# Two sums over channels by a pair of fp32r products, and the layer norm's mean one unit later

## The chip, the cores and the metric

The kernel runs on one core of one Trainium2 chip. The metric is the time of one execution on the device, in microseconds (us). The engines are called as the profile calls them: PE is TensorE (matrix products), PEld its weight load, DVE is VectorE, ACT is ScalarE, POOL is GpSimd and SP is SyncE, which here issues most of the transfers. PSUM is the memory that TensorE accumulates into; it is handed out in banks of 128x512 fp32.

## The reference

One encoder layer over 512 positions of 2048 channels, in fp32. After an RMS norm one projection feeds two groups: a convolution module with a layer norm, and neighbourhood attention with 16 heads. Each group's output is divided by its root mean square, and both go through one output projection. A gated MLP follows.

```
h = u_val * sigmoid(u_gate)
h = depthwise_conv(h, dw_w, dw_b)                # width 31, 1024 channels
mu = mean(h); var = mean(square(h - mu))         # over channels
y_conv = silu((h - mu) * rsqrt(var + EPS) * ln_g + ln_b)

y_na = neighborhood_attention(q, k, v, rpb)      # 1024 channels
mixed = concat(rms_norm(y_conv, conv_out_g), rms_norm(y_na, na_out_g))
x = x + mixed @ w_out
x = x + (silu(gate) * val) @ w_down              # from x's norm, w_up and a width-3 convolution
return rms_norm(x, final_norm_g)
```

The change touches the mean of the layer norm, and the root mean square of the attention's output.

## The kernel before, in words

Activations stand with channels on the 128 partitions and the 512 positions along the free side, so 1024 channels are eight tiles of 128x512. A mean over channels is therefore a sum over tiles, done by VectorE, and then a sum over partitions, done by TensorE with a matrix of ones.

**Products.** Weights come as raw fp32 units of 128x1024. ScalarE makes a high part in the format fp32r (L130), VectorE the rest (L131). Activations are split in the same way. A unit of the projections is 24 products of 128x512: high by high and high by low for eight tiles, alternating (L147, L148), then low by high (L150). The first projection takes two such units for one block of 128 output columns, the output projection one (`out_half`, L602), first for the convolution's half and then for the attention's.

**Steps between units.** What lies between projections, such as attention, layer norm and roots, is written as coroutines. `tick` (L157) is called behind the last product of each unit; it runs the coroutine at the head of `steps` and the one at the head of `asteps` up to their next `yield`. So a `yield` moves what follows it one unit later. Attention of a head pair is such a coroutine in `steps`: scores, some units later the transposes of the softmax (L522), a unit later the products with the values (L538). `group_a`, in `asteps`, is the layer norm and what follows it: the sum of the eight convolution tiles (L426, L428), the mean (L431, L433), deviations and squares (L436, L437), the inverse root of the variance, normalising, swish and the split of the operands (L443 to L445), and five units later the group's own root (`ra`, L451). `norm_b` (L614) makes the attention group's root `rna` from `acc_na`, the sum of its squares.

**Order.** A planner puts the instructions of each engine in order when the program is built, by their places in the program (moved by `shifted`), by their dependences and by its own estimates of time; it also hands out the buffers. `issue_after` and `pin` bind the order in places. On the chip each engine then runs its list in that order.

**Roots.** `rsqrt_steps` (L254) sums over partitions with a narrow product for each block of 128 positions (L258), so that positions come to lie on partitions. `root_steps` makes the inverse root on tiles of 128x4 (L233 to L240), builds diagonal blocks (L245), and a unit later spreads them over all partitions with two products of ones (L249) and a copy (L251).

**Buffers.** `stat` (L222) takes PSUM for such sums from a tile of two banks with the tag `sc`, which is shared with attention's scores, transposes and value products; there is one of it. Projections rotate through three banks (`psm`). A unit of the output projection is read from its bank when `ra` is there (`read_a`, L617 to L623), in the second half with `rna` (L652). Small tiles of 128x512 come from a pool of 75. Weights are loaded into nine buffers, four of which hold the convolution's results until the layer norm has read them.

Of the kernel before, what the change touches and what calls it, by code (L numbers as in the profile page):

```python
# [10 lines left out]
F32 = mybir.dt.float32  # L11
F32R = mybir.dt.float32r
AF = mybir.ActivationFunctionType
ALU = mybir.AluOpType
AX = mybir.AxisListType

P = 128
D = 2048
S = 512
# [4 lines left out]
NA = 1024  # L24
# [4 lines left out]
EPS = 1e-6  # L29
# [49 lines left out]
def layer(ctx: ExitStack, tc: tile.TileContext, xT, xn, xw, w_0, w_in, w_out, w_up, w_down, par, tab, g3, out):  # L79
    nc = tc.nc  # L80
# [6 lines left out]
    psa = ctx.enter_context(tc.tile_pool(name="psa", bufs=1, space=bass.MemoryType.PSUM))  # L87
# [9 lines left out]
    def t2(name, dt=F32):  # L97
        return tp.tile([P, S], dt, tag="t2k", name=name)
# [8 lines left out]
    def pc(name, i):  # L107
        o = POFF[name] + i
        return prm[:, o:o + 1]

    ones_r = consts.tile([P, P], F32R, name="ones")
    ones = ones_r.bitcast(F32)
# [3 lines left out]
    ps = psm.tile([P, S], F32, tag="mm", name="warm")  # L116
# [5 lines left out]
    def raw_unit(src, n):  # L122
        raw = t4([P, U * P], "raw")
        return raw, nc.sync.dma_start(raw[:, :n], src)
# [82 lines left out]
    def split(src, g, name):  # L207

        h, l = t2(name + "h", F32R), t2(name + "l", F32R)
        nc.scalar.activation(h, src, AF.Copy, scale=g)  # L210
        nc.vector.scalar_tensor_tensor(l, src, g, h.bitcast(F32), op0=ALU.mult, op1=ALU.subtract)
        return h, l

    def sum_sq(acc, src, first, to=slice(0, S)):
        if first:
            nc.scalar.activation(acc, src, AF.Square)
        else:
            q = t2("sq")[:, to]
            nc.scalar.activation(q, src, AF.Square)
            nc.vector.tensor_add(acc, acc, q)  # L220

    def stat():  # L222
        if where:
            return psa.tile([P, S], F32, tag="tr", name="st", bufs=2)
        return psa.tile([P, 2, S], F32, tag="sc", name="st")[:, 0]
# [3 lines left out]
    def root_steps(sums, n, name, bank=None):  # L229

        v, r, y = (sm.tile([P, S // P], F32, tag="rs" + c, name="rs" + c) for c in "vry")
        h = sm.tile([P, S // P], F32R, tag="rsh", name="rsh")
        nc.vector.tensor_scalar(v, sums, 1.0 / n, EPS, op0=ALU.mult, op1=ALU.add)  # L233
        nc.scalar.activation(r, v, AF.Sqrt)
        nc.vector.tensor_mul(y, r, r)
        nc.vector.tensor_add(y, y, v)
        nc.vector.reciprocal(y, y)
        nc.vector.scalar_tensor_tensor(y, y, 2.0, r, op0=ALU.mult, op1=ALU.mult)
        nc.vector.tensor_copy(h, y)
        nc.vector.tensor_sub(v, y, h.bitcast(F32))  # L240

        dg = [t2("dg", F32R) for _ in range(2)]
        for d, x in zip(dg, (h.bitcast(F32), v)):
            for i in range(S // P):
                nc.vector.tensor_scalar(d[:, i * P:(i + 1) * P], ident, x[:, i:i + 1], None, op0=ALU.mult)  # L245
        yield
        ps = bank() if bank else stat()
        for i in range(2):
            nc.tensor.matmul(ps, ones_r, dg[i], start=i == 0, stop=i == 1)  # L249
        res = t2(name)  # L250
        nc.scalar.activation(res, ps, AF.Copy)  # L251
        return res

    def rsqrt_steps(acc, n, name, bank=None):  # L254

        ps = stat()
        for i in range(S // P):
            nc.tensor.matmul(ps[:, i:i + 1], acc[:, i * P:(i + 1) * P], ones[:, 0:1], start=True, stop=True)  # L258
        return (yield from root_steps(ps[:, :S // P], n, name, bank))


    xs, x1 = [], []
    pin = tc.keep_in_program_order

# [25 lines left out]
    for k in range(ROWS):  # L290
        n = 3 * P
# [8 lines left out]
        else:  # L300
            his = [t2("weh", F32R)[:, :P], t2("weh", F32R)[:, P:n]]
            h, l = t2("xh", F32R), t2("xl", F32R)
# [22 lines left out]
    for u in range(2):  # L325
        raw, i = raw_unit(w_in[1, :, u * U * P:(u + 1) * U * P], U * P)
# [8 lines left out]
    for step in ORDER:  # L335
        i = next(a_ if step == "a" else q_)
# [84 lines left out]
    def group_a():  # L421
        yield
        while taps:
            yield
        acc = t2("acc")
        nc.vector.tensor_add(acc, ys[0], ys[1])  # L426
        for i in range(2, NC_):
            nc.vector.tensor_add(acc, acc, ys[i])  # L428
        yield
        ps = psa.tile([P, 2, S], F32, tag="sc", name="st")[:, 0]  # L430
        nc.tensor.matmul(ps, ones, acc, start=True, stop=True)  # L431
        mu = t2("mu")
        nc.vector.tensor_scalar(mu, ps, 1.0 / CONV, None, op0=ALU.mult)  # L433
        acc = t2("acc")
        for i in range(NC_):
            nc.vector.tensor_sub(ys[i], ys[i], mu)  # L436
            sum_sq(acc, ys[i], i == 0)  # L437
        yield
        yield
        r = yield from rsqrt_steps(acc, CONV, "rln")  # L440
        acc = t2("acc")
        for i in range(NC_):
            nc.vector.tensor_mul(ys[i], ys[i], r)  # L443
            nc.scalar.activation(ys[i], ys[i], AF.Silu, scale=pc("lng", i), bias=pc("lnb", i))
            ma.append(split(ys[i], pc("cog", i), "ma"))  # L445
        for i in range(NC_):
            sum_sq(acc, ys[i], i == 0)
        for _ in range(RA_AFTER):
            yield

        ra.append((yield from rsqrt_steps(acc, CONV, "ra",  # L451
                                          lambda: psa.tile([P, S], F32, tag="po", name="st"))))


    mb, rb = [], []
    acc_na = t2("accna")
# [123 lines left out]
    p, n = -1, 0  # L580
    for step in ORDER:
        if step == "a":
            if n < 2:
                with tc.issue_after(last.ins):
                    glu(n) if n else first_glu()
            else:
                glu(n)
            n += 1
            continue
        p += 1  # L590
        steps.append(attend(p, *qkv(p)))
        if p == NORM_AT:
            asteps.append(group_a())
# [18 lines left out]
    wait = []  # L612

    def norm_b():  # L614
        rb.append((yield from rsqrt_steps(acc_na, NA, "rna")))

    def read_a(d, ps):  # L617
        wait.append((d, ps))
        while ra and wait:
# [3 lines left out]
            nc.vector.tensor_add(x2[d], x2[d], t)  # L623

    steps.append(norm_b())
    assert len(ma) == NC_
    out_half(ma, read_a)
# [465 lines left out]
```

## Time and profile before

| what | us |
|---|---|
| median of 3 runs | 1960.12 |
| lowest and highest | 1960.04 and 1960.94 |
| the profiled execution | 1960.14 |
| its span in the trace | 1958.4 |
| TensorE busy | 1948.2 (99%) |
| VectorE busy | 1605.9 (82%) |
| ScalarE busy | 1084.3 (55%) |

The span is the time between the first and the last recorded instruction; the execution's time has 1.74 us around it. A row of the chain gives a start, a length and the work; a row of a timeline adds the idle time of the engine ahead of it, with what ended that. A row of the windows gives a stretch, its length, and the busy times of TensorE, its weight load, VectorE, ScalarE and POOL, then the granted clock and the load of the transfers. A row of waits gives who waited for whom, the total, how often and the longest.

### The profile page before, as it was taken

The numbers are of one execution on the slowest core, as the hardware profiler recorded it, in microseconds if no ns is written. First come the engines' busy times: TensorE is split into PE (matmuls) and PEld (weight loads), VectorE is DVE, ScalarE is ACT, GpSimd is POOL, SyncE is SP. The second block draws the span as 40 slices with busy tenths as digits, with TensorE's granted clock in tenths as the row PEclk, the third lists the DMA queues.
The fourth block names the chain that finished last, engine by engine and source line by source line (L and its number), as shares of the span: only waits on it lengthen the run. The fifth ranks groups of instructions, "written<-read, shape, count | busy, mean of one in ns | idle before, by whom it ended". The sixth has DMA issues, their size and how long they took to land.

```text
span 1958.4 us, 28132 instructions
## 1 busy us (share of the span) xinstructions
PE 1948.2 (99%) x10391; PEld 1657.4 (85%) x10391; DVE 1605.9 (82%) x2348; ACT 1084.3 (55%) x1724; POOL 225.8 (12%) x310
## 2 busy tenths in 40 slices
PE   9999999999999999999999999999999999999998
PEld 8888888888888888888888888888888888888886
DVE  5988688887548888888888888898989898885764
ACT  6244423448426666666666666666666644554654
POOL 0111111110011111111111111111111300000000
PEclk9999999999999999999999999999999999999999
DMA  9677677677768899999999999999996967666663
GB/s 372 177 188 182 188 190 182 184 182 234 240 161 218 198 258 253 267 249 265 246 264 249 263 257 255 259 253 259 252 259 166 389 233 234 218 215 194 192 204 118
DMA packets 141531, 448.92 MB, mean 229 GB/s; under 512 B 14928, under 2 KB 27216, under 8 KB 139984
## 3 DMA queue, kind: packets, MB, share of 16 engines
q1 hardware_dynamic: 89168, 291.90, 44.0%
q0 software_dynamic: 42624, 148.92, 35.4%
q10 hardware_dynamic: 9600, 6.29, 1.1%
q8 instruction: 82, 1.34, 0.3%
q14 instruction: 57, 0.47, 0.1%
HBM read 428.17 MB, written 111.15 MB: 275 GB/s over the span
## 4 chain that ended last, share of the span: by engine, by line
PE 99%; DVE 1%; issue 0%; ACT 0%; DVEq 0%
PE pu L749 44%; PE pd L888 21%; PE pj L147 7%; PE pj L148 7%; PE pj L150 7%; PE po L147 3%; PE po L148 3%; PE po L150 3%; PE pj L386 1%; PE po L538 1%; PE pj L390 1%; PE sc L497 1%; PE trp L522 1%; PE trx L644 0%; DVE acc L428 0%
## 5 line engine op out<-in xcount | busy, mean ns | idle before, releaser
L130 ACT ACTIVATE whi<-raw 128x1024 fp32r<-128x1024 f32 (+1 forms) x574 | 604.3, 1054 | 535.8 <-PE pj L148 134.6
L131 DVE TENSOR_TENSOR wlo<-raw,whi 128x1024 fp32r<-128x1024 f32 (+1 forms) x574 | 698.9, 1218 | 221.4 <-ACT whi L130 194.1
L749 PE MATMUL pu<-xc,whi 128*128 128x512 f32 x2464 | 593.6, 391 | 0.0
L749 PEld LDWEIGHTS pu<-xc,whi 128*128 128x128 f32 x2464 | 451.3, 188 | 86.7 <-DVE xc L637 0.4
L749 PEld LDWEIGHTS pu<-xc,wlo 128*128 128x128 f32 x2464 | 319.2, 191 | 13.7
L749 PE MATMUL pu<-xc,wlo 128*128 128x256 f32 x2464 | 324.2, 283 | 0.0
L888 PE MATMUL pd<-whi,ho 128*128 128x512 f32 x1232 | 305.1, 389 | 0.0
L888 PEld LDWEIGHTS pd<-whi,ho 128*128 128x128 f32 x1232 | 231.1, 188 | 48.7 <-DVE vl L762 0.5
L147 PE MATMUL pj<-xh,whi 128*128 128x512 f32 x592 | 233.2, 394 | 0.0
L148 PE MATMUL pj<-xl,whi 128*128 128x512 f32 x592 | 230.8, 390 | 0.0
L413 DVE SCALAR_TENSOR_TENSOR y<-ch,prm,y 128x500 f32<-128x500 f32 (+14 forms) x240 | 177.1, 741 | 5.3
L888 PE MATMUL pd<-wlo,ho 128*128 128x512 f32 x616 | 165.1, 389 | 0.0
L150 PE MATMUL pj<-xh,wlo 128*128 128x512 f32 x592 | 146.2, 389 | 0.0
L888 PEld LDWEIGHTS pd<-wlo,ho 128*128 128x128 f32 x616 | 115.6, 188 | 24.1
L147 PEld LDWEIGHTS pj<-xh,whi 128*128 128x128 f32 x592 | 111.1, 188 | 25.7 <-issue 2.7
L148 PEld LDWEIGHTS pj<-xl,whi 128*128 128x128 f32 x592 | 111.2, 188 | 23.1 <-issue 0.2
L150 PEld LDWEIGHTS pj<-xh,wlo 128*128 128x128 f32 x592 | 111.1, 188 | 23.1
L758 ACT ACTIVATE pu<-pu 128x512 f32<-128x512 f32 x132 | 76.5, 580 | 93.2 <-PE pu L749 93.1
L698 POOL DMA_DIRECT2D raw<-in_w_up x88 | 78.2, 889 | 355.2 <-DVE wlo L131 194.0
L202 POOL DMA_DIRECT2D ws<-in_w_down x88 | 79.5, 904 | 301.8 <-DMA ws<-in_w_down 119.3
L199 POOL DMA_DIRECT2D ws<-in_w_down x44 | 23.3, 529 | 312.9 <-PE pj L150 178.0
L199 POOL DMA_DIRECT2D ws<-ws x44 | 23.2, 527 | 311.8 <-PE pj L150 96.3
(198 smaller groups left out, 1949.4 us busy)
## 6 DMA issues: line engine op xcount, KB each, us to landing
raw<-in_w_up SPq DMA_DIRECT2D x220, 512.0 KB, 5.9
ws<-in_w_down POOLq DMA_DIRECT2D x132, 512.0 KB, 6.4
raw<-in_w_up POOLq DMA_DIRECT2D x88, 512.0 KB, 7.4
raw<-ws SPq DMA_DIRECT2D x88, 512.0 KB, 3.7
raw<-in_w_in SPq DMA_DIRECT2D x74, 512.0 KB, 5.4
raw<-in_w_down SPq DMA_DIRECT2D x66, 512.0 KB, 3.7
ws<-ws POOLq DMA_DIRECT2D x44, 512.0 KB, 5.7
raw<-in_w_out SPq DMA_DIRECT2D x32, 512.0 KB, 5.6
```

Source lines behind the costliest of these rows:

```text
L130: i = nc.scalar.activation(hi[:, :n], raw[:, :n], AF.Copy)
L131: j = nc.vector.tensor_sub(lo[:, :n], raw[:, :n], hi[:, :n].bitcast(F32))
L147: nc.tensor.matmul(ps, hi, mh, start=first and k == 0, stop=False)
L148: nc.tensor.matmul(ps, hi, ml, start=False, stop=False)
L150: i = nc.tensor.matmul(ps, lo[:, wk * P:(wk + 1) * P], mh, start=False, stop=last and k == len(ws) - 1)
L199: behind(nc.gpsimd.dma_start(wsum[c][k], a), ins)
L202: nc.gpsimd.dma_start(wsum[c][k], w_down[k, {1: A21, 2: A11, 4: A11, 6: A12}[c]], accum_op=ALU.add, max_dma_last_dim=ROW)
L413: nc.vector.scalar_tensor_tensor(y[:, a:b], h[:, a + j - PAD:b + j - PAD], prm[:, o:o + 1], y[:, a:b], op0=ALU.mult, op1=ALU.add)
L698: nc.gpsimd.dma_start(a[c], w_up[f, q2], accum_op=ALU.add)
L749: i = nc.tensor.matmul(ps[:, :n], part[:, k * P:(k + 1) * P], comb[c][k][:, :n], start=j == 0 and not more, stop=j == 2 * U - 1, skip_grou ...
L758: nc.scalar.activation(to, ps, AF.Copy)
L888: m = nc.tensor.matmul(ps[i], h[:, o + t * P:o + (t + 1) * P], w[:, d], start=start and not more and kind == 0 and j == 0, stop=stop and k ...
```

## The change

The sum over partitions of an fp32 tile is made from two fp32r products instead of one fp32 product. `halved` makes a high part (ScalarE) and the rest (VectorE); `column_sums` multiplies both by the matrix of ones into one bank, so that every partition holds the sum. The mean of the layer norm uses this, with one more `yield` between the making of the halves and the products. The attention output's root uses it too, in `roots_of_sums`, in place of narrow products, work on 128x4 and the spreading pair: the root is now worked out on 128x512, with the same formula. The other roots stay.

```diff
+    def halved(src):
+        h, l = t2("ah", F32R), t2("al", F32R)
+        nc.scalar.activation(h, src, AF.Copy)
+        nc.vector.tensor_sub(l, src, h.bitcast(F32))
+        return h, l
+
+    def column_sums(two):
+        ps = stat()
+        for i in range(2):
+            nc.tensor.matmul(ps, ones_r, two[i], start=i == 0, stop=i == 1)
+        return ps
+
+    def roots_of_sums(acc, n, name):
+        two = halved(acc)
+        yield
+        ps = column_sums(two)
+        v, r, y = t2("v"), t2("r"), t2(name)
+        nc.vector.tensor_scalar(v, ps, 1.0 / n, EPS, op0=ALU.mult, op1=ALU.add)
+        nc.scalar.activation(r, v, AF.Sqrt)
+        nc.scalar.activation(y, r, AF.Square)
+        nc.vector.tensor_add(y, y, v)
+        nc.vector.reciprocal(y, y)
+        nc.vector.scalar_tensor_tensor(y, y, 2.0, r, op0=ALU.mult, op1=ALU.mult)
+        return y
...
@@ group_a
             nc.vector.tensor_add(acc, acc, ys[i])
+        two = halved(acc)
         yield
-        ps = psa.tile([P, 2, S], F32, tag="sc", name="st")[:, 0]
-        nc.tensor.matmul(ps, ones, acc, start=True, stop=True)
+        yield
+        ps = column_sums(two)
         mu = t2("mu")
...
@@ norm_b
-        rb.append((yield from rsqrt_steps(acc_na, NA, "rna")))
+        rb.append((yield from roots_of_sums(acc_na, NA, "rna")))
```

## The prediction

> **What bounds the kernel now.** I read the page first (engine totals, then the chain that ended last), then TensorE's waits, then the chain in three short stretches around the lines that the diff touches, and last the timelines of VectorE, ScalarE and SyncE there.
>
> ```profile
> span 1958.4 us, 28132 instructions
> PE 1948.2 (99%) x10391; PEld 1657.4 (85%) x10391; DVE 1605.9 (82%) x2348; ACT 1084.3 (55%) x1724; POOL 225.8 (12%) x310
> PE 99%; DVE 1%; issue 0%; ACT 0%; DVEq 0%
> ```
> ```profile
> PE warm L118 <- DVE ones L113: 1.1, 1, 1.1
> PE st L431 <- DVE acc L428: 0.6, 1, 0.6
> ```
>
> TensorE is the chain: 99% of it. Its whole list of waits has two entries, and one of them is a line that the diff replaces. So only two things can move the time: the length of what TensorE executes, and a wait that is removed from it or given to it. Work on VectorE, ScalarE or a queue costs nothing until it turns into a third entry in that list.
>
> **The change part by part.** First the mean of the layer norm. The chain between 423 and 432 us, and the same product in TensorE's timeline:
>
> ```profile
> 425.57 0.70 DVE acc L428
> ...
> 426.41 1.10 PE st L431 x2
> ```
> ```profile
> 426.41 1.10 PE L431 MATMUL st<-acc,ones 128*128 128x512 f32 x2 [0.58 <-DVE acc L428]
> ```
>
> The full fp32 product of 128x512 takes 1.10 us of TensorE, and TensorE stands 0.58 us ahead of it because the last addition of acc ends at 426.27, when the projection unit ahead has been through since 426.41 - 0.58 = 425.83. The new form of a column sum exists already in this program: L249 accumulates two fp32r products with the same matrix of ones. The chain around the attention output's root, with such a pair in its second half:
>
> ```profile
> 536.38 0.79 PE st L258 x8
> 537.17 0.35 PE po L147
> ...
> 540.96 1.82 PE po L150 x8
> 542.78 0.47 PE st L249 x2
> 543.25 0.23 PE po L147
> ```
>
> The pair costs 0.47 us, and the product behind it starts at its usual pace (0.23). So the mean goes from 0.58 + 1.10 = 1.68 to 0.47: minus 1.21 us, if its operands are there. They should be: the products come one unit later, and a unit is 24 products of 1.82 / 8 = 0.227, so 5.44 us; what is added ahead of them is one ScalarE copy and one VectorE subtraction of 128x512 (0.60 and 0.68, by the L251 and L220 rows below), done by 428 or 429 even with a weight subtraction in between, while the unit of that place ends at 425.83 + 5.44 = 431.3.
>
> [...]
>
> Second, the attention output's root. Today it is eight narrow products (L258, 0.79), the next projection product starts slower behind them (0.35 instead of 0.23: 0.12), and a unit later comes the pair that spreads the root over the partitions (0.47): 1.38 in all. Afterwards one pair stands for both: 0.47. Minus 0.91 us, with no wait to be removed in it.
>
> What the other engines get for that root:
>
> ```profile
> L237 DVE RECIPROCAL rsy<-rsy 128x4 f32<-128x4 f32 x5 | 0.9, 178 | 0.2
> L511 DVE RECIPROCAL su<-su 128x2 f32<-128x2 f32 x32 | 4.9, 158 | 6.2 <-ACT s L510 6.1
> ```
> ```profile
> 543.29 0.60 ACT L251 ACTIVATE rna<-st 128x512 f32<-128x512 f32 x1 [1.18 <-PE st L249]
> ```
> ```profile
> 438.44 0.68 DVE L220 TENSOR_TENSOR acc<-acc,sq 128x512 f32<-128x512 f32 x1
> 542.82 0.69 DVE L622 TENSOR_TENSOR oa<-po,ra 128x512 f32<-128x512 f32 x1 [1.44 <-PE po L150]
> 548.76 0.69 DVE L622 TENSOR_TENSOR oa<-po,ra 128x512 f32<-128x512 f32 x1 [2.92 <-PE po L150]
> 581.40 0.69 DVE L652 TENSOR_TENSOR oa<-po,rna 128x512 f32<-128x512 f32 x1 [3.02 <-PE po L150]
> ```
>
> ScalarE gets three passes of 0.60 for one of 0.60 and a tiny root. VectorE loses seven small steps and eight diagonal blocks, and gets four full-width steps (0.7 each) and a full-width reciprocal. No row shows a reciprocal of 128x512: its low end is an ordinary step, 0.69; its high end goes by the slope from 2 to 4 columns, (178 - 158) / 2 = 10 ns a column, so 5.1 us. I take the high end as the more careful one. Either way it hides: the root is first read by L652 at 581.40, 37 us after today's root is ready (543.29 + 0.60). What is queued behind it on VectorE is L622 of the unit at hand and a weight subtraction. L622 frees a PSUM bank; there are three, so a 5.1 us delay of one stays below the two units (10.9 us) before that bank is wanted again. If that cover were gone, the price would be the reciprocal itself, 5.1 us.
>
> [...]
>
> Third, what the extra unit moves: everything in the layer norm's coroutine behind the mean. The rows that set its slack:
>
> ```profile
> 438.44 1.31 PE trp L522 x12
> 440.21 0.90 PE st L258 x8
> 446.27 1.38 PE po L538 x38
> 449.47 0.46 PE st L249 x2
> 477.78 0.79 PE st L258 x8
> 484.18 1.31 PE trp L522 x12
> 485.49 0.47 PE st L249 x2
> 496.88 1.37 PE po L538 x38
> ```
> ```profile
> 427.54 0.69 DVE L433 TENSOR_SCALAR mu<-st 128x512 f32<-128x512 f32 x1
> 441.15 0.16 DVE L233 TENSOR_SCALAR rsv<-st 128x4 f32<-128x4 f32 x1 [2.03 <-PE st L258]
> 444.19 0.87 DVE L245 TENSOR_SCALAR dg<-ident,rsv 128x128 fp32r<-128x128 f32 x4
> 448.35 0.69 DVE L575 TENSOR_TENSOR ao<-ao,po 128x512 f32<-128x512 f32 x1 [0.42 <-ACT ao L574]
> 464.29 0.75 DVE L211 SCALAR_TENSOR_TENSOR mal<-y,prm,mah 128x512 fp32r<-128x512 f32 x1
> 487.04 0.69 DVE L622 TENSOR_TENSOR oa<-po,ra 128x512 f32<-128x512 f32 x1 [2.36 <-ACT ra L251]
> ```
> ```profile
> 481.21 0.79 ACT L513 ACTIVATE s<-s,su 128x192 f32<-128x192 f32 x2
> ```
> ```profile
> 472.20:477.80 5.60, 5.60 (x28) 4.67 (x26) 5.60 (x13) 5.59 (x18) 0.51 (x1) 1.00 1.04 397
> ```
>
> The mean's step moves from 427.54 to about 431.8 (unit end 431.3, products 0.47), 4.3 us later. Squares and sums behind it end at 438.44 + 0.68 + 4.3 = 443.4. The narrow sums of the layer norm's variance (L258 at 440.21) now fall behind attention's value products, whose two-bank tile they share: it is free when L575 ends, 449.04 - 1.21 = 447.8, so they land inside the unit at about 448. Their root took from 441.15 to 445.06, 3.9 us; so the diagonal blocks are done near 453 and the spreading pair, at 449.47 today only because it too waited for that tile, goes to about 453: 3.5 to 5 us later. The normalised operands then end at 464.29 + 0.75 + 5 = 470 at most, and the output projection reads the first of them at 478.57 - 1.21 = 477.4 (478.57 is 477.78 + 0.79). Seven microseconds of slack: cost nothing. The second root (L258 at 477.78, L249 at 485.49) moves a unit too; its consumer L622 goes from 487.04 to about 492.5. The fourth output unit needs the PSUM bank that L622 empties; its first product stands at 498.25 (496.88 + 1.37), 497.0 after the gain. Slack 4.5 us: nothing.
>
> SyncE and the queues. The moved steps issue no transfers, but the convolution's results sit in four of the nine buffers that weights are loaded into, and they are let go when these squares end.
>
> ```profile
> 446.82 20.30 SPq L124 DMA_DIRECT2D raw<-in_w_out  x6
> 467.83 1.91 SPq L546 DMA_DIRECT2D tab<-in_tab  x2
> 472.99 7.28 SPq L124 DMA_DIRECT2D raw<-in_w_out  x5
> 480.36 16.13 SPq L599 DMA_DIRECT2D x<-in_xT  x16
> ```
>
> Eleven output weights are on their way by 480.27, when the output projection has only started on the first; five microseconds later, or the last five behind the residual's loads (480.36 + 16.13 = 496.5), still brings the seventh in soon after 500, and its unit starts six units after 477.4, at 510. Nothing again. POOL's weight sums hang on unit ends alone and are not passed.
>
> Waits that the trace of before cannot show: three groups of products get new neighbours (the mean's pair, L258 of the variance, L258 of the second root). Low end: the present L258 at 440.21 took 0.90 against 0.79 elsewhere, so 0.11 may vanish. High end: each could stand as L431 does today, 3 x 0.58 = 1.7. I take zero, since five of the seven groups of such products in the rows above show none (all but L431 and L258 at 440.21).
>
> Sum: -1.21 - 0.91 = -2.12. Against the profiled execution (span 1958.4, time 1960.14, so 1.74 around it): 1956.3 and 1958.0. The median of the runs is 1960.12, the same within 0.02. That is 0.11% faster, and about 0.2% (3.9 us) is what a measurement of this kernel can tell from no change; I call that the same.
>
> **The rivals.** *The last softmax but one is late.* Behind the layer norm in ScalarE's and VectorE's order stands the softmax of head pair 6; its last scaling ends at 482.00 and the transposes that read it start at 484.18. Slipped by 3.6 to 5 us it ends at 485.6 to 487.0, while TensorE is there at 483.0: a wait of 2.6 to 4.0, time 1960.6 to 1962.0. For it: in the row from 472.2 to 477.8, VectorE is busy for 5.60 and ScalarE for 5.59 of 5.60 us, so nothing there catches up. Against it: the planner need not keep the place; it already lets the value products of that pair slide a unit (496.88, two units behind their transposes).
>
> *Slower: the fourth output unit waits for its PSUM bank.* The second root slips not one unit but three (16.3 us), because its narrow sums queue for the shared two-bank tile behind the late transposes. L622 then comes at 503.3 instead of 497.0: plus 6.3, time 1964.3. It decides from a slip of 10 us on and reaches the slower verdict at 16. For it: tile and banks are shared just there. Against: one unit and the late softmax together make 9.4 at most.
>
> *Faster by over 0.2%.* It would need 3.9 us; all the products touched, taken away whole, are 1.68 + 1.38 = 3.06. Only a different order elsewhere could give the rest.
>
> *The change does nothing:* the mean's pair stands as L431 does (0.58) and the two other moved groups too: 1959.7. I count it in the forecast's range.
>
> **How the numbers follow.** Forecast 0.66 (1957.4 to 1959.8); late softmax 0.17 (1960.6 to 1962.0); slower 0.13; faster 0.04. Predicted time 1958.0. The range runs from 1957.0 to 1962.0, which leaves out the last two and little else. Chances: faster 0.04, within 0.2% 0.66 + 0.17 = 0.83, slower 0.13.
>
> **What would show it.** Right: TensorE's list of waits has no entry for the mean; two pairs of about 0.47 on the new line; the stretch of 536 to 543 has no narrow sums and no 0.35 behind them; the first L622 near 492. Wrong: a new entry of over 1 us in that list between 440 and 505 (transposes: the softmax; an output product: the bank), or a reciprocal far beyond 5.1 us with L622 behind it. A change outside 410 to 580 us would mean that the order moved where I looked at nothing.

## The result, and the profile after

The changed kernel takes 1966.37 us (median, 1965.78 to 1966.95) against 1960.17 us: slower by 6.2 us, ratio 1.0031 with a 95% interval of 1.0022 to 1.0039. The forecast was 1958.0 with a range of 1957.0 to 1962.0.

The page of the kernel after, its totals and its chain:

```profile
span 1964.5 us, 28107 instructions
PE 1949.6 (99%) x10383; PEld 1658.7 (84%) x10383; DVE 1610.5 (82%) x2339; ACT 1085.5 (55%) x1726; POOL 225.4 (11%) x310
PE 97%; DVE 1%; ACT 1%; issue 0%; DVEq 0%
```

TensorE is 97% of the chain where it was 99%. Its list of waits says where the rest went (who waits, for whom, total, times, longest):

```profile
PE po L147 <- DVE oa L651: 4.2, 1, 4.2
PE warm L118 <- DVE ones L113: 1.1, 1, 1.1
PE st L249 <- DVE dg L245: 1.0, 2, 0.7
PE po L567 <- DVE rsv L233: 0.3, 1, 0.3
```

The wait at the mean is gone, as forecast. In its place there are three entries, 5.5 us together, all at the convolution group's own root: an output product waits for the reader of its bank (L147), the spreading pair for the diagonal blocks (L249), and the value products for the step that reads the narrow sums (L567 for L233). L651 is the line that was L622, the multiplication by `ra` that empties an output unit's PSUM bank. TensorE's timeline there:

```profile
431.45 0.39 PE L273 MATMUL st<-ah,ones 128*128 128x512 f32 x1
...
482.05 0.82 PE L551 MATMUL trp<-ident,s 128*128 128x128 f32 x6
482.62 0.47 PE L147 MATMUL po<-mah,whi 128*128 128x512 f32 x1
483.24 0.33 PE L551 MATMUL trp<-ident,s 128*128 128x128 f32 x1
...
494.69 0.95 PE L258 MATMUL st<-ones,acc 128*128 128x1 f32 x8
495.99 1.44 PE L567 MATMUL po<-pt,vt 64*64 64x64 f32 x48 [0.35 <-DVE rsv L233]
498.12 0.51 PE L249 MATMUL st<-dg,ones 128*128 128x512 f32 x1 [0.69 <-DVE dg L245]
498.91 0.50 PE L249 MATMUL st<-dg,ones 128*128 128x512 f32 x1 [0.28 <-DVE dg L245]
503.64 0.79 PE L147 MATMUL po<-mah,whi 128*128 128x512 f32 x1 [4.24 <-DVE oa L651]
504.23 0.63 PE L148 MATMUL po<-mal,whi 128*128 128x512 f32 x1
504.66 0.63 PE L147 MATMUL po<-mah,whi 128*128 128x512 f32 x1
```

The copy that makes `ra` on ScalarE, and the reader on VectorE:

```profile
501.77 0.57 ACT L251 ACTIVATE ra<-st 128x512 f32<-128x512 f32 x1
502.90 1.28 DVE L651 TENSOR_TENSOR oa<-po,ra 128x512 f32<-128x512 f32 x2
```

The narrow sums of the second root stood at 477.62 in the same timeline before (477.78 in the chain) and stand at 494.69 now. Two full output units lie between the first transposes of head pair 6 and these sums. The fourth output unit starts at 503.64 instead of 498.19, and its bank's reader at 502.90, where it was at 487.04. And its products follow each other at 0.43 instead of 0.23 us: 504.23, 504.66. The windows say why (stretch, length, busy TensorE, weight load, VectorE, ScalarE, POOL, then the granted clock):

```profile
500.00:504.00 4.00, 0.36 (x1) 0.36 (x2) 4.00 (x6) 1.72 (x3) 0.00 (x0) 0.64 1.05 390
504.00:508.00 4.00, 4.00 (x10) 3.10 (x10) 3.72 (x6) 0.00 (x0) 0.00 (x0) 0.51 0.66 269
508.00:512.00 4.00, 4.00 (x27) 3.18 (x29) 0.53 (x1) 1.21 (x2) 0.31 (x1) 1.00 0.42 137
```

Behind the wait TensorE is granted half its clock for about four microseconds. In that time ten products run (x10 in the second row), where twenty did in the 4.00 us from 500.00 of the kernel before: some 2 us.

The account, by the starts of the same products in both timelines. At the first output product the changed kernel is 1.8 us ahead, half of it because the second root's sums are not done yet. From there to the fourth output unit it loses 0.9 for these sums, 5.6 in the four waits of the timeline (0.35, 0.69, 0.28, 4.24), and 0.7 that no single row carries, where transposes and the spreading pair stand among other products: 5.4 behind. The lowered clock makes it 7.4. The attention root gives 1.0 back, 6.4, and at the end of the span it is 6.1.

### The profile page after: what moved, and what is told of

It is laid out like the page before. It is cut to its first block, busy times and chain, and to the rows that moved or that the text cites. A ratio compares the mean times of both kernels' runs of the same rounds, so it can differ in the third digit from the quotient of the medians.

```text
span 1964.5 us, 28107 instructions
## 1 busy us (share of the span) xinstructions
PE 1949.6 (99%) x10383; PEld 1658.7 (84%) x10383; DVE 1610.5 (82%) x2339; ACT 1085.5 (55%) x1726; POOL 225.4 (11%) x310
## 4 chain that ended last, share of the span: by engine, by line
PE 97%; DVE 1%; ACT 1%; issue 0%; DVEq 0%
PE pu L778 44%; PE pd L917 21%; PE pj L147 7%; PE pj L148 7%; PE pj L150 6%; PE po L147 3%; PE po L148 3%; PE po L150 3%; PE pj L414 1%; PE pj L418 1%; PE sc L526 1%; PE trp L551 1%; PE po L567 0%; PE trx L673 0%; ACT y L473 0%
## 5 line engine op out<-in xcount | busy, mean ns | idle before, releaser
L147 PE MATMUL pj<-xh,whi 128*128 128x512 f32 x592 | 232.7, 393 | 0.0
L147 PEld LDWEIGHTS pj<-xh,whi 128*128 128x128 f32 x592 | 111.1, 188 | 25.5 <-issue 2.5
```

Of the source, the lines that this page charges most:

```text
L147: nc.tensor.matmul(ps, hi, mh, start=first and k == 0, stop=False)
```

## The experiments

**One part alone.** Two kernels undo one half of the change each.

The mean as changed, the attention root as before:

```diff
-        rb.append((yield from roots_of_sums(acc_na, NA, "rna")))
+        rb.append((yield from rsqrt_steps(acc_na, NA, "rna")))
```

> Theory (the bank): the extra unit in the layer norm makes the convolution group's root so late that the fourth output unit waits about 4 us for its PSUM bank, and TensorE then runs at half clock for some 4 us; the attention root's pair has no part in it. This kernel has the mean's pair and the extra unit, and the attention root as before: it keeps the wait and lacks the root's gain of 0.9, so about 1967.3 us. Rival (the wide root): the full-width reciprocal and its neighbours on VectorE hold something up; then the loss is gone here and the time is about 1959.0 (1960.2 minus 1.2).

Measured: 1966.93 us (1966.82 to 1967.57), ratio 1.0035 (1.0021 to 1.0048). Its trace has the same wait as the change, to the tenth:

```profile
PE po L147 <- DVE oa L651: 4.2, 1, 4.2
```

The attention root as changed, the mean as before:

```diff
-        two = halved(acc)
-        yield
         yield
-        ps = column_sums(two)
+        ps = psa.tile([P, 2, S], F32, tag="sc", name="st")[:, 0]
+        nc.tensor.matmul(ps, ones, acc, start=True, stop=True)
```

> The attention root by the pair, the mean as before. The bank theory: no long wait of TensorE, 1960.2 minus 0.9 = 1959.3 us, the wait of 0.6 at the mean's fp32 product still there. The rival of the wide root: a wait after 540 us in the trace and a time of 1964 us or more. The reciprocal of 128x512 should show between 0.7 and 5.1 us.

Measured: 1959.24 us (1958.93 to 1959.91) against 1960.21 in the same comparison, ratio 0.9996 (0.9987 to 1.0004). The size is the forecast one, 1.0 us for 0.9, though the interval of the ratio takes in no change. TensorE's waits are those of the kernel before, and the reciprocal of full width is in VectorE's timeline:

```profile
546.67 3.35 DVE L286 RECIPROCAL rna<-rna 128x512 f32<-128x512 f32 x1
549.93 0.63 DVE L650 TENSOR_TENSOR oa<-po,ra 128x512 f32<-128x512 f32 x1
```

It takes 3.35 us, between the two ends of the prediction (0.69 and 5.1), and the bank's reader L650 queues behind it without anybody waiting. So the wide root is not the cause.

**The unit alone.** The kernel before, with one `yield` more and no pair at all:

```diff
         yield
+        yield
         ps = psa.tile([P, 2, S], F32, tag="sc", name="st")[:, 0]
```

> The kernel before with one more unit between the sum of the convolution tiles and the mean's single fp32 product, and nothing else. The bank theory: the unit alone is the cause, so the fourth output unit waits about 4 us, TensorE's clock halves behind it, and the time is that of the mean's pair with the extra unit plus the 0.6 us that the fp32 product is longer: about 1967.9 us. A rival, that the pair (its high part on ScalarE, its low part on VectorE) pushes the later steps: then this kernel gains the 0.6 us wait and loses nothing, about 1959.6.

Measured: 1967.61 us (1966.22 to 1968.13), ratio 1.0036 (1.0023 to 1.0048), with this in the trace:

```profile
PE po L147 <- DVE oa L623: 4.2, 1, 4.2
```
```profile
504.00:508.00 4.00, 3.83 (x9) 3.09 (x10) 4.00 (x7) 0.00 (x0) 0.00 (x0) 0.50 0.75 303
```

The one line is enough for the wait and for the lowered clock. The loss is the extra unit's, not that of the pairs.

**The pairs without the unit.**

```diff
         two = halved(acc)
         yield
-        yield
         ps = column_sums(two)
```

> Both pairs as in the change, but without the extra unit before the mean's products. The bank theory: the convolution group's root keeps its old place, no output unit waits, and the two gains remain: 1960.2 minus 2.1 = 1958.1 us if the halves are there in time, up to 1958.7 if TensorE waits 0.6 for them. Rivals in which the pairs or the wide root are at fault: 1962 us or more.

Measured: 1959.30 us (1958.89 to 1959.97), ratio 0.9995 (0.9986 to 1.0004). The bank's wait is gone. TensorE now waits for the halves, which the expectation had put at up to 0.6, and there is a short wait more at the variance's sums:

```profile
PE warm L118 <- DVE ones L113: 1.1, 1, 1.1
PE st L273 <- ACT ah L265: 0.7, 1, 0.7
PE st L258 <- DVE acc L220: 0.2, 1, 0.2
```

The time is 1.2 us above 1958.1, of which these rows carry 0.9, and 0.6 above the 1958.7 that the expectation allowed. So the extra unit had a use: it covers the making of the halves.

**The unit kept, and taken back one step later.** The change, with the second root four units behind its operands:

```diff
-RA_AFTER = 5
+RA_AFTER = 4
```

> The change with the convolution group's own root four units after its operands instead of five, which undoes the extra unit for that root alone; the layer norm stays a unit later. The bank theory: the root's narrow sums stand ahead of the late transposes again, the fourth output unit does not wait, the clock stays at 1.0: 1960.2 minus 2.1 = 1958.1 us, up to 1959 with short waits at the split transposes. Rival (the late softmax or the late operands cost TensorE time by themselves): a wait stays between 476 and 500 and the time is 1961 or more.

Measured: 1958.25 us (1957.57 to 1958.67) against 1960.14, ratio 0.9989 (0.9980 to 0.9998). All of TensorE's waits that are left are the one at the start:

```profile
PE warm L118 <- DVE ones L113: 1.1, 1, 1.1
```
```profile
477.02 1.02 PE L258 MATMUL st<-ones,acc 128*128 128x1 f32 x8
483.48 0.93 PE L551 MATMUL trp<-ident,s 128*128 128x128 f32 x7
```
```profile
490.23 0.69 DVE L651 TENSOR_TENSOR oa<-po,ra 128x512 f32<-128x512 f32 x1 [1.22 <-ACT ra L251]
```

The narrow sums stand ahead of the transposes again, and the bank's reader is at 490.23, where it was at 487.04 before and at 502.90 in the change. Of the prediction's sum of 2.1 us, 1.9 are there. This kernel is 8 us faster than the change, and 1.9 us faster than the kernel before, which the interval of the ratio just tells from no change.

**How much lateness does it take?** The kernel before, with nothing late but the second root:

```diff
-RA_AFTER = 5
+RA_AFTER = 6
```

> The kernel before with the convolution group's root six units after its operands instead of five: this root alone is a unit later, the mean and the softmax stay. Theory: one unit alone is within the slack of 11 us that the bank has (its reader at 487.0, the fourth unit at 498.2), so the root slips 5 to 6 us and the time stays at 1960.2, within 0.6. It takes the softmax of head pair 6 being late as well, so that the narrow sums lose the shared two-bank tile to its transposes, to slip three units. Rival (any delay of this root by a unit brings the wait): 1965 us or more.

Measured: 1963.84 us (1961.73 to 1964.18), ratio 1.0016 (1.0007 to 1.0025). This expectation missed, and its rival of 1965 or more did not come either. The trace:

```profile
482.91 1.47 PE L522 MATMUL trp<-ident,s 128*128 128x128 f32 x12
...
491.07 0.95 PE L258 MATMUL st<-ones,acc 128*128 128x1 f32 x8
...
500.25 0.50 PE L147 MATMUL po<-mah,whi 128*128 128x512 f32 x1 [1.93 <-DVE oa L622]
```

The step moved by one unit of 5.44 us and its sums by 13.5 (477.62 to 491.07), though the softmax was not late here: the transposes stand whole at 482.91. So the sums come far behind these transposes without any lateness of the softmax. ScalarE's copies had emptied the tile by 483.77 + 1.64 = 485.4; the sums' place, 5.7 us later, is that of the order.

The times of this kernel fall into two groups, three near 1961.8 and eight near 1963.9 us; the profile is of the first, in which the clock stays at 1.00 behind the wait. It was run once more for that.

> The kernel of the root a unit later once more, for its profile: its times fell into two groups, three near 1961.8 and eight near 1963.9 us, and the profile was of the first. Theory: the wait of 1.9 us is the same in both, and in the second TensorE's granted clock drops behind it for some 4 us, worth the 2.1 us. Rival: in the second group the wait itself is 2 us longer and the clock stays at 1.0.

Measured: 1961.75, again of the first group, wait and clock as in the profile above. What the second group does was not seen in a profile. Its mean granted clock is 0.998 against 0.999 of the first, which could be worth 2 us over the span. But these figures are rounded: two runs of the kernel with the attention root alone have the same two clocks and the same time (1959.52 and 1959.58 us). So neither the clock nor a longer wait is shown to be the cause.

**What holds the sums back?** The change, with the narrow sums in the bank that the spreading pair uses, instead of attention's two-bank tile:

```diff
     def rsqrt_steps(acc, n, name, bank=None):
-        ps = stat()
+        ps = bank() if bank else stat()
```

> The change, with the narrow sums of the convolution group's root in the bank that its spreading pair uses already, not in the two-bank tile that attention shares. If that tile is what holds the narrow sums, they come at about 483 instead of 494.9. The spreading pair does not move by itself: it stood behind the value products of head pair 6 at about 497, so the root is ready near 499 and the fourth output unit waits 1 to 2 us instead of 4.2, too short for a long drop of the clock: 1960 to 1963 us. If the tile is not what holds them, the time is that of the change, 1966.4.

Measured: 1963.16 us (1962.39 to 1963.81), ratio 1.0015 (1.0006 to 1.0024). TensorE, then VectorE:

```profile
482.08 0.82 PE L551 MATMUL trp<-ident,s 128*128 128x128 f32 x6
482.73 0.95 PE L258 MATMUL st<-ones,acc 128*128 128x1 f32 x8
...
495.32 1.44 PE L567 MATMUL po<-pt,vt 64*64 64x64 f32 x48
496.69 0.74 PE L249 MATMUL st<-dg,ones 128*128 128x512 f32 x2
500.95 0.63 PE L147 MATMUL po<-mah,whi 128*128 128x512 f32 x1 [3.52 <-DVE oa L651]
```
```profile
487.67 0.87 DVE L245 TENSOR_SCALAR dg<-ident,rsv 128x128 fp32r<-128x128 f32 x4
...
497.46 0.69 DVE L604 TENSOR_TENSOR ao<-ao,po 128x512 f32<-128x512 f32 x1 [0.76 <-ACT ao L603]
498.94 0.75 DVE L211 SCALAR_TENSOR_TENSOR mbl<-ao,prm,mbh 128x512 fp32r<-128x512 f32 x1 [0.79 <-ACT mbh L210]
499.61 0.68 DVE L220 TENSOR_TENSOR accna<-accna,sq 128x512 f32<-128x512 f32 x1
500.21 1.28 DVE L651 TENSOR_TENSOR oa<-po,ra 128x512 f32<-128x512 f32 x2
```

In that bank the sums are at 482.73 instead of 494.69: that they share the two-bank tile is what puts them so late in the order. But it is not the whole delay. The diagonal blocks are ready at 488.5, and the spreading pair stands at 496.69 all the same, behind the value products of head pair 6; and behind the pair the reader queues on VectorE after what those products bring (L604, L211, L220), 3.5 us more. The wait only falls from 4.24 to 3.52; I had expected 1 to 2, and the time is just above the 1960 to 1963 expected. The place of the pair was settled when the program was ordered, and no run here shows by which estimate.

**More of the same?** The convolution group's root by a pair as well, on top of the extra unit:

```diff
-RA_AFTER = 5
+RA_AFTER = 2
...
-        ra.append((yield from rsqrt_steps(acc, CONV, "ra",
-                                          lambda: psa.tile([P, S], F32, tag="po", name="st"))))
+        ra.append((yield from roots_of_sums(acc, CONV, "ra")))
```

> The change with the convolution group's own root made by a pair as well, and two units after its operands instead of five, so that its sums stand at the end of the first output unit. It drops the eight narrow products there (0.79 and the slow product behind them, 0.12). The bank theory: the wide root takes VectorE and ScalarE some 8 us, its reader comes near 493, the fourth output unit starts near 497 without a wait, the clock stays: 1958.25 (the change with its root one unit sooner) minus 0.9 = 1957.3 us. If the wide root is too slow, the bank's wait is back: 1959 to 1962.

Measured: 1960.21 us (1959.82 to 1961.63), ratio 1.0001 (0.9992 to 1.0010): no gain over the kernel before, 2 us above the version with RA_AFTER at 4, and not the 1957.3 expected. The bank is not waited for; the halves are, since ScalarE has their high part ready only at about 483.4 (the subtraction that reads it starts at 483.41), behind steps of the softmax. The profile is of a run of 1961.59 us:

```profile
PE st L273 <- ACT ah L265: 1.7, 1, 1.7
PE warm L118 <- DVE ones L113: 1.1, 1, 1.1
PE st L273 <- DVE al L266: 0.2, 1, 0.2
PE po L147 <- DVE k L494: 0.2, 1, 0.2
```

## Why the prediction was wrong

**The sum of the change itself** was right. The mean's pair stands at 431.45, where the prediction had the unit's end at 431.3, and TensorE does not wait for its operands. The pair for the attention root gives 1.0 us alone (0.9 forecast). The two together, with the second root put back ahead of the transposes, give 1.9 of the 2.1.

**The layer norm's slack** was right too: in the chain its narrow sums stand at 447.56 and its spreading pair at 452.78 (about 448 and 453 forecast), and no entry in TensorE's list is for the normalised operands, which the prediction had 7 us early.

**The step that failed** is the sentence on the second root: that it "moves a unit too", its consumer going "from 487.04 to about 492.5", with 4.5 us of slack to the fourth output unit. It went to 502.90. I gave a step that is moved by one `yield` a delay of one unit. But that one unit put it from ahead of the transposes of head pair 6 to behind them, and there the order gave its narrow sums a late place, because they share the two-bank tile, and its spreading pair one behind the value products. Three runs put sizes on it: 477.62 to 491.07 with the root alone late, to 494.69 with the layer norm late as well, and back to 482.73 once the sums had another bank. The place that the order gave them is not where the tile comes free on the chip: ScalarE had copied the last of the transposes by 484.13 + 1.60 = 485.7,

```profile
484.13 1.60 ACT L559 ACTIVATE pt<-trp 128x384 f32<-128x384 f32 x4
495.87 0.20 ACT L234 ACTIVATE rsr<-rsv 128x4 f32<-128x4 f32 x1 [8.84 <-DVE rsv L233]
```

and then, but for a table load, did nothing: 8.84 us idle until the sums of that root were through. So the tile lay unused from 485.7 to 494.69, while TensorE ran output units.

**The rival that came true** is the slower one, with its chance of 0.13. Its place is right, and its sizes nearly: the sums slip 17.1 us for the 16.3 foreseen, the reader comes at 502.90 for 503.3, and the fourth output unit waits for its bank. Of its mechanism the shared tile is right, but the late softmax is not needed: the root alone, one unit later, slips 13.5 us behind transposes that are on time. Its argument against itself, that a unit and the late softmax "together make 9.4 at most", was the same mistake. Its price of 1964.3 lacked the lowered clock, 2.0 us. The other rival, the late softmax, did come late (its last scaling ends at 484.2, where it was 482.00) but cost no wait: the transposes were split, six at 482.05 and six more among the products behind.

**The clock** was not in the prediction at all. In the trace of the change, in windows of 0.25 us, the granted clock falls to 0.50 at 501.1 (0.72 in the window from 501.00, 0.50 in the next), 1.7 us after the long wait began (503.64 - 4.24 = 499.40), and is back at 1.00 at 507.9 (0.63 in the window from 507.75, 1.00 in the next): half clock for 6.8 us, 4.3 of them behind the wait. With the sums in the other bank the windows of 4 us have 0.64 from 500 and 0.93 from 504; if the clock was 1.00 or 0.50 and nothing between, that is half clock from about 501.1, right behind the wait of 3.52 us, to 504.6, about 3.4 us. The products agree: they follow each other at 0.43 us from 500.95 to 504.36 and at about 0.23 from 504.69 on. Shortly ahead of the fall in the change TensorE was not without work: it ran the two products of the spreading pair, at 498.12 and 498.91, 1.0 us together. That a wait of 1 to 2 us is too short for a long drop, as the expectation of the other bank has it, was my estimate, and the runs do not agree on it. For the wait of 1.93 us the two profiles at hand show no drop; whether the second group of that kernel's times, 2.1 us longer, has one stays open. Behind the wait of 1.67 us in the kernel with the convolution group's pair, twelve transposes took 2.57 us (1.47 with the root alone late), and products from 488.41 to 489.26 followed each other at 0.43 us, the pace of the half clock in the change; of its granted clock only the 1.00 from 490 on is known.

## What to carry to other kernels

Where an order is computed and small steps share a buffer with large ones, a step moved by one slot may land on the other side of a large one: count its delay from the place where it comes to stand, with the buffers that it must wait for there, and not from the slot. Look for the last reader that empties a PSUM bank, and keep its margin in view, since the waits of TensorE of 3.52 and 4.24 us cost about half as much again in clock (the unit behind them took 7.17 and 7.58 us, 5.62 before). A part of the schedule that is moved for one step's sake can sometimes be moved back a step later, as the one number RA_AFTER did here.

## What the runs showed of the hardware

The reciprocal of 128x512 fp32 on VectorE took 3.35 us, five times an ordinary step of that size (0.68). In the change the half clock came with the wait of 4.24 us, lasted 4.3 us behind it and cost 2.0; with the wait of 3.52 us the granted clock was 0.64 from 500 to 504. The two other kernels with a wait of 4.2 us (the mean's pair with its unit, and the unit alone) show the same drop, to 0.50 in the window from 504 to 508. The clock fell 1.7 us into the wait of 4.24 us, with short waits of 0.69 and 0.28 us ahead of it; a wait of 1.93 us showed no drop in two profiles.
